# Two-layer hybrid decoder trunk: the second layer's mixer pacing, the order of its input blocks, S5's output products, and one modulation section

## The chip, the core and the metric

The kernel runs on one core of a Trainium2 chip as one launch. The metric is the device time of one execution in microseconds (us). TensorE (PE, with its weight loads shown apart as PEld), VectorE (DVE), ScalarE (ACT), GpSimd (POOL) and SyncE (SP) run their own instruction streams in order; the whole order is written out when the program is built.

## The reference, cut to what matters

```python
for l in range(2):
    sh1, sc1, gt1, sh2, sc2, gt2 = split(silu(c) @ ada_w[l] + ada_b[l], 6)   # "modulation"
    a = rms_norm(h, norm1_g[l]) * (1 + sc1) + sh1
    u_s5, r_q, r_k, r_v, r_g, w_q, w_k, w_v, m_cq, m_ckv, m_kr = split(a @ w_in[l])
    y = concat(s5(u_s5), retention(r_*), sliding_window(w_*), mla(m_*))      # 4 mixers, 512 wide each
    h = h + gt1 * (y @ w_out[l])
    a = rms_norm(h, norm2_g[l]) * (1 + sc2) + sh2
    h = h + gt2 * (square(relu(a @ mlp_w1[l])) @ mlp_w2[l])
out = rms_norm(h, final_norm_g)
# s5: u -> B u (complex, 16 tiles of 128 states) -> scan over 256 steps -> Re(C state) + d u -> gelu -> GLU
```

One sequence of 256 positions, width 2048, all float32. MLA is the latent attention (two low-rank projections, rotary, softmax), SWA the windowed attention with sinks, RET the retention mixer.

## The kernel before

**The data stream.** `make_plan` (L84) writes one list of items. A data item is a 128x1024 float32 slab of weights (128x640 for block K) that SP fetches from one packed stream, in list order. For an "in", "out", "w1" or "w2" item ScalarE rounds the slab to a high part `wH` and VectorE subtracts to get a low part `wL` (`prep`, L350); `NHL` = 3 such pairs exist, so both run up to three items ahead of TensorE, which then does three matmuls for each product (high by high, high by low, low by high). An "ad" item belongs to the modulation: VectorE multiplies the slab by silu(c) and sums it, TensorE does nothing. "aquad" entries make the normalised activations of 512 channels in stages: products with a diagonal matrix on TensorE, scale and shift on ScalarE, the low part on VectorE.

**The second layer's order.** Norm, then 56 "in" items, 8 for each of the blocks U (S5's input), C, K, Q, RQK, RV, RG; then 32 "out" items. Before, the items of U and C alternate by quarter of the contraction, and the aquads of quarters 1 to 3 are spread over these 16 items by `AQ` (L80). The sixteen "ad" items of the shift SH2 are merged into the 48 items from RV on.

**The mixers.** They are Python generators (`s5` L1423, `mla` L1021, `swa` L971, `ret` L1167) that issue a few instructions and yield. Each "in" or "out" item calls `step()` (L410) twice, once for each half of its matmuls; a call is named a slot here. A slot lets S5 go first, one turn, then the others one turn each, in rotation, until the `Meter` (L225) has counted more than the budget `BUD` (L252) in that slot: VectorE 3, ScalarE 3, TensorE 1.5 in the second layer. The meter counts 0.07 + 0.00104 n for a VectorE instruction on n elements per partition. Where a result is needed, `ysplit` (L799) calls `need` (L432), which calls `step()` until that mixer is done, with no data item in between: MLA is needed before the first output item, SWA before the third, S5 before the seventh, RET before the eleventh.

**S5.** For each of 8 pairs of state tiles: products with B (4 matmuls, `bu`), two turns that multiply by cosine and sine, a turn with half the scan and its carry, a turn with the other half, two turns that multiply back, and the output products of the pair (8 matmuls into the bank `yp`, L1514 to L1522), which are issued right after them. Every second pair then adds the skip term. Before the fifth pair seven turns make the tables' second half (`s5_steps`).

Of the kernel before, what the change touches and what calls it, by code (L numbers as in the profile page):

```python
# [13 lines left out]
ALU = mybir.AluOpType  # L14
# [33 lines left out]
def _merge(main, extra):  # L48
    out, e, n, m = [], 0, len(main), len(extra)
    for i, it in enumerate(main):  # L50
        out.append(it)
        want = (i + 1) * m // n
        out.extend(extra[e:want])
        e = want
    return out
# [9 lines left out]
def _ad_sec(l, s, n=16):  # L65
    return [("ad", l, s, j, hf) for j in range(n) for hf in range(2)] + [("modfin", l, s, n)]
# [10 lines left out]

AQ = sorted([(max(0, 2 * k - 1 + stage), k, stage) for k in range(6) for stage in range(3)], reverse=True)  # L80
AQ = [(at, 1 + k // 2, 2 * (k % 2), stage) for at, k, stage in AQ]


def make_plan():  # L84
    p = []
    for l in range(LAYERS):
# [26 lines left out]
        else:  # L113
            p += _gap(1, 1)
            rest = REST[1]
        if l == 1:
            pair = rest[:2]
            first = [("in", l, b, kq, hf) for kq in range(4) for b in pair for hf in range(2)]
            rest = first + [("in", l, b, kq, hf) for b in rest[2:] for kq in range(4) for hf in range(2)]
        else:  # L120
            rest = [("in", l, b, kq, hf) for b in rest for kq in range(4) for hf in range(2)]
        if l == 0:
            rest = _merge(rest, later[4:]) if rest else later[4:]
        QO = MIX[l]
        outs = [("out", l, q, nb, hf, q == QO[0] and hf == 0, q == QO[3] and hf == 1)
                for nbs in ((0, 1), (2,), (3,)) for q in QO for nb in nbs for hf in range(2)]
        if l == 1:
            for at, q, c, stage in AQ:
                rest.insert(at, ("aquad", l, 1, q, c, stage))
            at = rest.index(("in", l, "RV", 0, 0))  # L130
            ws = rest[at:] + outs
            ws = _merge(ws[:48], _ad_sec(1, SH2, 8)) + ws[48:]
            rest = rest[:at] + ws
            rest.insert(at - 4, ("csilu", l))
            rest.insert(at - 4, ("cload", l))
        else:
            rest += outs
            rest.insert(len(rest) - 4, ("csilu", l))
            rest.insert(len(rest) - 16, ("cload", l))
        at = rest.index(outs[0])  # L140
        rest[at:at] = [("hload", l), ("gput", l, GT1)]
        rest.insert(rest.index(outs[10]), ("gget", l, GT1))
# [8 lines left out]
        w += [("w1", l, nb, kq, hf) for nb in range(2, 16) for kq in range(4) for hf in range(2)]  # L151
        w += [("w2", l, kq, nb, hf) for kq in range(16) for nb in range(4) for hf in range(2)]
        if l == 0:
            ex = _ad_sec(0, GT2) + sum([_ad_sec(1, s, 8 if s == SH1 else 16) for s in (SC1, SH1, GT1, SC2)], [])
        else:
            ex = _ad_sec(1, GT2)
        ex.append(("cdone", l))
# [87 lines left out]
def trunk_kernel(ctx: ExitStack, tc: tile.TileContext, A, out):  # L245
# [3 lines left out]

    NHL, NS, LA = 3, 31, 4  # L250

    BUD = ((1, 1.5, 1), (3, 3, 1.5))  # L252
    cst = ctx.enter_context(tc.tile_pool(name="cst", bufs=1))
    hp = ctx.enter_context(tc.tile_pool(name="hp", bufs=1))
    whp = ctx.enter_context(tc.tile_pool(name="whp", bufs=NHL))
# [23 lines left out]
    def bank():  # L279
        assert banks, "no bank left"  # L280
        tag = banks.pop(0)
        uid[0] += 1
        t = ps.tile([128, 512], F32, tag=tag, name=f"p{uid[0]}")
        owner[id(t)] = (tag, t)
        return t
# [9 lines left out]
    def g_banks(n, reserve=2):  # L295
        while len(banks) < n + reserve:
            yield
# [97 lines left out]

    bud = [BUD[0]]

    def run_bg(name, gen):
        active.append((name, gen))

    rr, nslot, pace = [0], [0], [2]

    def step1(a):
        try:
# [5 lines left out]
    def step():  # L410

        v0, a0, p0 = V.t, ACT.t, PE.t
        lead = [a for a in active if a[0][0] in ("T", "S5")]
        rest = [a for a in active if a[0][0] not in ("T", "S5")]
        nslot[0] += 1
        if nslot[0] % pace[0]:
            return
        if rest:
            r = rr[0] % len(rest)
            rest = rest[r:] + rest[:r]  # L420
        for i, a in enumerate(lead + rest):
            if i >= len(lead):
                rr[0] += 1
            step1(a)
            if V.t - v0 > bud[0][0] or ACT.t - a0 > bud[0][1] or PE.t - p0 > bud[0][2]:
                break

    def g_wait(n):
        for _ in range(n):
# [993 lines left out]
    def s5(l):  # L1423
# [29 lines left out]
        yield from g_banks(2, 1)  # L1453
        nxt = bu(0)
        yield
        yp = None
        for p in range(8):
            pbs = nxt
            if p == 4:
# [19 lines left out]
            if p < 7:  # L1479
                yield from g_banks(2, 1)  # L1480
                nxt = bu(p + 1)
            mg = [mag[:, 2 * p + e:2 * p + e + 1].to_broadcast([128, 128]) for e in range(2)]
            for e in range(2):
                for r in range(2):
# [21 lines left out]
            for e in range(2):  # L1506
# [3 lines left out]
                V.tensor_tensor(P8[:, 0:4, :], w4, cosb, op=ALU.mult)  # L1510
                V.tensor_tensor(P8[:, 4:8, :], w4, sinb, op=ALU.mult)
                yield
            yield
            if p % 2 == 0:  # L1514
                yield from g_banks(1, 1)
                yp = bank()
            for n, (m, src) in enumerate(((0, 0), (0, 3), (1, 2), (1, 1))):
                for e in range(2):
                    i = 2 * p + e
                    p0, cs, o = 32 * (i % 4), slice(32 * i, 32 * i + 32), 256 * (n == 3)  # L1520
                    PE.matmul(yp[p0:p0 + 32, o:o + 256], lhsT=C[:, m, cs], rhs=W[2 + e][:, src, :],
                              start=n in (0, 3), stop=n in (2, 3), tile_position=(0, p0))  # L1522
            if p % 2 == 1:
                yield
                k = p // 2
                V.scalar_tensor_tensor(y[:, k, :], u[:, k, :], T["d"][:, 0, k:k + 1], yp[:, 0:256],
                                       op0=ALU.mult, op1=ALU.add)
                V.tensor_tensor(y[:, k, :], y[:, k, :], yp[:, 256:512], op=ALU.subtract)
                bfree(yp)
        free(C, bT, cos, sin, *W)  # L1530
        yield from g_slots(3)
        gw = [slot([128, 2, 512]) for _ in range(2)]
# [230 lines left out]
```

## Time and profile before

| | |
|---|---|
| median of 3 runs | 2331.61 us (2330.83 to 2331.77) |
| the profiled execution: time / span of its instructions | 2330.54 us / 2328.4 us |
| granted TensorE clock, mean | 0.991 |
| HBM traffic | 252 GB/s over the span |
| matmul records | 12150 |

The page of the profile gives the busy time of each engine. The granted clock is a share of full speed: 1.00 is the 2.4 GHz level and 0.50 the 1.2 GHz level, and a value between is a stretch that had both. An entry in brackets at the end of a timeline row is the engine's idle time just before that instruction and what released it. Two records stand for one float32 matmul (w by w), one for one matmul of the rounded parts.

### The profile page before, as it was taken

Reading aid. Unit: us, or ns where it says so; the run is one execution under the profiler, and the core shown is the slowest. Engines: PE = TensorE matmul, PEld = TensorE weight load, DVE = VectorE, ACT = ScalarE, POOL = GpSimd, SP = SyncE. Lnnn points to the kernel's source line nnn. Section 1 sums busy time; section 2 is a strip of 40 time slices with the busy share of each in tenths; the row PEclk is TensorE's granted clock in tenths of the full one; section 3 lists DMA queues with packets and bytes.
Section 4 is the critical chain, followed back from the end, with each engine's and each line's share of the span. In section 5 each row is a group of like instructions: output and inputs, shape, how many; then the busy total and the mean of one; then the engine's idle time right before and its main releaser. Section 6 shows DMA issues by size and latency. Waiting matters only on the chain.

```text
span 2328.4 us, 32118 instructions
## 1 busy us (share of the span) xinstructions
PE 2254.6 (97%) x12150; PEld 1809.9 (78%) x12150; DVE 1579.4 (68%) x2591; ACT 1016.7 (44%) x1378; POOL 40.9 (2%) x65
## 2 busy tenths in 40 slices
PE   6999999999999999999999889999999999999997
PEld 3775457889888888888878757778988888888885
DVE  5848764646878787889965987574576665545546
ACT  2352245544444444444444345544444444444443
POOL 0000000000000000000000000000000000000000
PEclk9999999999999999999999989999999999999999
DMA  9986677777888889998985314787667766667640
GB/s 380 408 329 244 253 290 269 273 272 260 281 280 286 271 307 334 339 335 296 342 315 196 97 57 154 262 320 277 215 223 236 233 214 202 216 215 221 219 146 36
DMA packets 162459, 588.23 MB, mean 253 GB/s; under 512 B 18448, under 2 KB 18672, under 8 KB 162304
## 3 DMA queue, kind: packets, MB, share of 16 engines
q1 hardware_dynamic: 156096, 563.79, 68.6%
q0 software_dynamic: 6208, 22.39, 2.9%
q8 instruction: 95, 1.56, 0.3%
q14 instruction: 60, 0.49, 0.1%
HBM read 581.88 MB, written 4.23 MB: 252 GB/s over the span
## 4 chain that ended last, share of the span: by engine, by line
PE 84%; DVE 7%; issue 4%; DMA 2%; ACT 2%; POOL 0%; POOLq 0%; ACTq 0%; SPq 0%; DVEq 0%
PE p L239 84%; DVE w L239 5%; DVE wL L239 2%; DMA w<-in_stream_dram 2%; ACT wH L239 1%; ACT w L239 1%; DVE s5i L239 0%; ACT a L239 0%; DVE a L239 0%; DMA gains<-in_gains_dram 0%; POOL nr L569 0%; ACT rjk L239 0%; DVE f L239 0%; POOL rss L1232 0%; POOL mss L1038 0%
## 5 line engine op out<-in xcount | busy, mean ns | idle before, releaser
L239 DVE TENSOR_TENSOR wL<-w,wH 128x1024 fp32r<-128x1024 f32 (+1 forms) x688 | 831.9, 1214 | 612.7 <-ACT wH L239 602.7
L239 ACT CAST wH<-w 128x1024 fp32r<-128x1024 f32 (+1 forms) x688 | 715.9, 1044 | 931.9 <-PE p L239 798.7
L239 PE MATMUL p<-wH,a 128*128 128x512 f32 (+1 forms) x3200 | 1008.5, 390 | 11.6 <-ACT wH L239 6.6
L239 PE MATMUL p<-a,wH 128*128 128x512 f32 (+1 forms) x2880 | 838.2, 357 | 3.9 <-DVE a L239 2.6
L239 PEld LDWEIGHTS p<-wH,a 128*128 128x128 f32 x3200 | 600.4, 188 | 163.3 <-issue 22.1
L239 PE MATMUL p<-a,wL 128*128 128x256 f32 x2336 | 657.9, 282 | 4.2 <-DVE wL L239 4.2
L239 PE MATMUL p<-wL,a 128*128 128x512 f32 (+1 forms) x1600 | 618.6, 387 | 4.0 <-DVE wL L239 4.0
L239 PEld LDWEIGHTS p<-a,wH 128*128 128x128 f32 x2880 | 506.5, 189 | 100.2 <-ACT wH L239 7.2
L239 PEld LDWEIGHTS p<-a,wL 128*128 128x128 f32 x2336 | 442.9, 190 | 4.8 <-DVE wL L239 4.8
L239 PEld LDWEIGHTS p<-wL,a 128*128 128x128 f32 x1600 | 301.7, 189 | 64.3 <-DVE wL L239 7.0
L239 PE MATMUL p<-w,w 128*32 128x512 f32 (+5 forms) x1464 | 244.6, 507 | 10.6 <-DVE w L239 8.5
L239 DVE CUSTOM_DVE_ANT_0 w<-w,w 128x1024 f32<-128x1024 f32 x192 | 233.8, 1218 | 0.0
L239 PEld LDWEIGHTS p<-w,w 128*32 128x32 f32 (+3 forms) x1464 | 97.5, 134 | 109.9 <-issue 58.5
L239 ACT COPY w<-p 128x256 f32<-128x256 f32 (+2 forms) x192 | 85.7, 461 | 122.1 <-PE p L239 121.5
L239 DVE TENSOR_TENSOR w<-p,w 128x256 f32<-128x256 f32 (+1 forms) x230 | 113.2, 533 | 12.7 <-PE p L239 12.6
L239 DVE TENSOR_TENSOR w<-w,w 128x512 f32<-128x512 f32 (+6 forms) x172 | 93.6, 564 | 7.6 <-ACT w L239 4.0
L239 DVE TENSOR_TENSOR a<-w,a 128x1024 fp32r<-128x1024 f32 (+2 forms) x78 | 71.4, 918 | 10.6 <-ACT a L239 10.3
L239 ACT ACTIVATE w<-w 128x512 f32<-128x512 f32 (+2 forms) x50 | 36.9, 742 | 64.5 <-DVE w L239 62.0
L239 ACT CAST a<-w 128x1024 fp32r<-128x1024 f32 (+1 forms) x58 | 53.1, 916 | 0.6
L239 ACT COPY apev<-p 128x512 f32<-128x512 f32 x24 | 14.0, 584 | 50.9 <-PE p L239 50.9
L239 DVE SCALAR_TENSOR_TENSOR w<-w 128x1024 f32<-128x1024 f32 x28 | 34.3, 1226 | 1.0
L239 PEld LDWEIGHTS p<-kc,apev 128*128 128x128 f32 x192 | 23.4, 191 | 13.4 <-issue 4.2
(163 smaller groups left out, 639.4 us busy)
## 6 DMA issues: line engine op xcount, KB each, us to landing
w<-in_stream_dram SPq DMA_DIRECT2D x1056, 512.0 KB, 4.9
w<-in_stream_dram SPq DMA_DIRECT2D x16, 320.0 KB, 9.8
w<-gd POOLq DMA_DIRECT2D x8, 512.0 KB, 5.4
w<-in_w_uq_dram POOLq DMA_DIRECT2D x6, 384.0 KB, 7.5
w<-in_xT_dram SPq DMA_DIRECT2D x4, 512.0 KB, 6.9
w<-in_glu_w_dram POOLq DMA_DIRECT2D x4, 512.0 KB, 6.4
w<-in_x_dram POOLq DMA_DIRECT2D x4, 512.0 KB, 7.5
w<-in_c_dram POOLq DMA_DIRECT2D x4, 512.0 KB, 7.2
```

Source lines behind the costliest of these rows:

```text
L239: return f(out, *a, **k)
```

## The change

Four edits, all of them about the second layer but the last, which moves work of the second layer into the first layer's MLP.

1. The second layer's budget is VectorE 1.2, with a debt: what a slot spent is carried, each slot takes 1.2 off, and while a debt is left the slot issues nothing.
2. U's eight items come first, then C's; the aquads go by `AQ1`, one stage for each item, so that they are through after the first items.
3. S5's output products of a pair are issued in the next pair, after that pair's B products; for each odd pair two yields stand between its products and the skip term.
4. SH2's sixteen "ad" items go into the list that is merged into the first layer's MLP. With them gone, "cload" and "csilu" (the silu(c) rows for "ad" items) stand 16 and 4 items before the end of the output items, as in the first layer.

```diff
-AQ = sorted([(max(0, 2 * k - 1 + stage), k, stage) for k in range(6) for stage in range(3)], reverse=True)
-AQ = [(at, 1 + k // 2, 2 * (k % 2), stage) for at, k, stage in AQ]
+def _aq(step):
+    p = sorted([(max(0, step * k - 1 + stage), k, stage) for k in range(6) for stage in range(3)], reverse=True)
+    return [(at, 1 + k // 2, 2 * (k % 2), stage) for at, k, stage in p]
+AQ1, AQ = _aq(1), _aq(2)
...
-        if l == 1:
-            pair = rest[:2]
-            first = [("in", l, b, kq, hf) for kq in range(4) for b in pair for hf in range(2)]
-            rest = first + [("in", l, b, kq, hf) for b in rest[2:] for kq in range(4) for hf in range(2)]
-        else:
-            rest = [("in", l, b, kq, hf) for b in rest for kq in range(4) for hf in range(2)]
+        rest = [("in", l, b, kq, hf) for b in rest for kq in range(4) for hf in range(2)]
...
-            for at, q, c, stage in AQ:
+            for at, q, c, stage in AQ1:
                 rest.insert(at, ("aquad", l, 1, q, c, stage))
-            at = rest.index(("in", l, "RV", 0, 0))
-            ws = rest[at:] + outs
-            ws = _merge(ws[:48], _ad_sec(1, SH2, 8)) + ws[48:]
-            rest = rest[:at] + ws
-            rest.insert(at - 4, ("csilu", l))
-            rest.insert(at - 4, ("cload", l))
-        else:
-            rest += outs
-            rest.insert(len(rest) - 4, ("csilu", l))
-            rest.insert(len(rest) - 16, ("cload", l))
+        rest += outs
+        rest.insert(len(rest) - 4, ("csilu", l))
+        rest.insert(len(rest) - 16, ("cload", l))
...
-            ex = _ad_sec(0, GT2) + sum([_ad_sec(1, s, 8 if s == SH1 else 16) for s in (SC1, SH1, GT1, SC2)], [])
+            ex = _ad_sec(0, GT2) + sum([_ad_sec(1, s, 8 if s in (SH1, SH2) else 16)
+                                       for s in (SC1, SH1, GT1, SC2, SH2)], [])
...
-    BUD = ((1, 1.5, 1), (3, 3, 1.5))
+    BUD = ((1, 1.5, 1, False), (1.2, 3, 1.5, True))
...
         if nslot[0] % pace[0]:
             return
+        debt[0] = max(0.0, debt[0] - bud[0][0]) if bud[0][3] else 0.0
+        if debt[0] > 0:
+            return
...
+        debt[0] = V.t - v0
...
+        def out_products(p):
+            if p % 2 == 0:
+                yield from g_banks(1, 1)
+                yp[0] = bank()
+            for n, (m, src) in enumerate(((0, 0), (0, 3), (1, 2), (1, 1))):
...
+            if p % 2 == 1:
+                yield
+                yield
...
+                bfree(yp[0])
...
             if p < 7:
                 yield from g_banks(2, 1)
                 nxt = bu(p + 1)
+            if p:
+                yield from out_products(p - 1)
             mg = [mag[:, 2 * p + e:2 * p + e + 1].to_broadcast([128, 128]) for e in range(2)]
...
-            yield
-            if p % 2 == 0:
-                yield from g_banks(1, 1)
-                yp = bank()
-            for n, (m, src) in enumerate(((0, 0), (0, 3), (1, 2), (1, 1))):
...
-            if p % 2 == 1:
-                yield
...
-                bfree(yp)
+        yield
+        yield from out_products(7)
```

## Rows read from the trace of the kernel before

**Rows 1.** the page: busy time of each engine, share of the span, instructions.

```profile
PE 2254.6 (97%) x12150; PEld 1809.9 (78%) x12150; DVE 1579.4 (68%) x2591; ACT 1016.7 (44%) x1378; POOL 40.9 (2%) x65
```

**Rows 2.** 10-us windows: start:end, length, busy (count) by engine, PEclk, DMA share.

```profile
1280.00:1290.00 10.00, 8.96 (x71) 6.99 (x70) 9.93 (x27) 1.51 (x3) 0.00 (x0) 1.00 0.32 104
1290.00:1300.00 10.00, 8.96 (x69) 6.56 (x67) 9.93 (x18) 2.78 (x3) 0.00 (x0) 1.00 0.32 107
1300.00:1310.00 10.00, 8.70 (x69) 7.37 (x69) 9.93 (x31) 3.74 (x11) 1.53 (x1) 1.00 0.16 53
...
1320.00:1330.00 10.00, 6.90 (x40) 4.32 (x39) 9.56 (x24) 1.04 (x1) 0.36 (x1) 0.83 0.32 105
...
1350.00:1360.00 10.00, 3.64 (x11) 2.30 (x10) 6.91 (x34) 4.42 (x19) 0.00 (x0) 0.72 0.07 12
1360.00:1370.00 10.00, 7.52 (x27) 3.90 (x27) 6.21 (x18) 7.49 (x13) 0.00 (x0) 0.60 0.29 107
```

**Rows 3.** chain of waits, 1200 to 1560 us: start, us, what.

```profile
1214.05 56.48 PE p L239 x376
...
1368.99 107.62 PE p L239 x506
```

**Rows 4.** timeline of VectorE, one pair of S5: start, us, instruction [idle before, releaser].

```profile
1282.46 1.28 DVE L239 TENSOR_TENSOR w<-p,w 128x512 f32<-128x512 f32 x2
...
1286.44 0.82 DVE L239 TENSOR_TENSOR wL<-w,wH 128x640 fp32r<-128x640 f32 x1
...
1291.71 2.49 DVE L239 TENSOR_TENSOR w<-w,w 128x512 f32<-128x512 f32 x4
```

**Rows 5.** timeline of PE: output products of S5's first and second pair.

```profile
1281.26 2.08 PE L239 MATMUL p<-w,w 128*32 128x256 f32 x14 [1.04 <-DVE w L239]
...
1293.65 2.08 PE L239 MATMUL p<-w,w 128*32 128x256 f32 x14 [0.58 <-DVE w L239]
```

**Rows 6.** timeline of PE: 512-column matmuls after a stall and later.

```profile
1357.11 0.80 PE L239 MATMUL p<-wH,a 128*128 128x512 f32 x1 [5.90 <-ACT wH L239]
...
1371.01 0.50 PE L239 MATMUL p<-wH,a 128*128 128x512 f32 x1
```

**Rows 7.** timeline of POOL: MLA's second weight load; the residual's reload.

```profile
1397.71 0.53 POOL L1093 DMA_DIRECT2D w<-in_w_ukv_dram  x1 [63.29 <-DVE wL L239]
...
1471.49 1.68 POOL L1619 DMA_DIRECT2D w<-hs  x3 [9.26 <-ACT w L239]
```

**Rows 8.** timeline of PE at the first output item.

```profile
1480.74 0.80 PE L239 MATMUL p<-wH,a 128*128 128x512 f32 x1 [2.66 <-ACT a L239]
```

**Rows 9.** timeline of ScalarE: MLA's softmaxes, exponentials and division.

```profile
1445.54 0.40 ACT L239 ACTIVATE w<-w,sxm 128x128 f32<-128x128 f32 x1 [1.04 <-DVE sxm L239]
...
1449.01 0.19 ACT L239 ACTIVATION_READ_ACCUMULATOR w<-w,sxm 128x1 f32 x1
...
1455.94 2.87 ACT L239 ACTIVATE w<-w,sxd 128x128 f32<-128x128 f32 x8
```

**Rows 10.** timeline of VectorE: the maxima of the same softmaxes, first and last.

```profile
1444.38 0.28 DVE L239 CUSTOM_DVE_ANT_0 w<-p,kc 128x128 f32<-128x128 f32 x1
...
1446.80 0.08 DVE L239 DVE_READ_ACCUMULATOR2_ANT sxm<- 128x1 f32 x1
```

**Rows 11.** timeline of ScalarE: a table load and what follows.

```profile
1477.24 1.28 ACT L239 ACT_TABLE_LOAD   x1
1478.53 1.09 ACT L239 ACTIVATE w<-p 128x512 f32<-128x512 f32 x2
```

**Rows 12.** timelines of POOL and VectorE: the end of RET's chain.

```profile
1513.88 2.50 POOL L1232 TENSOR_TENSOR rss<-rss,mexp 128x8 f32<-128x8 f32 x1 [33.35 <-DVE rss L239]
...
1516.41 2.19 DVE L239 SCALAR_TENSOR_TENSOR w<-w,rss,w 128x128 f32<-128x128 f32 x8 [0.42 <-POOL rss L1232]
```

**Rows 13.** a window of the first layer's MLP.

```profile
1000.00:1200.00 200.00, 199.08 (x875) 163.78 (x874) 174.71 (x293) 86.38 (x89) 2.13 (x4) 1.00 0.88 318
```

**Rows 14.** a 10-us window at the first layer's first output items.

```profile
370.00:380.00 10.00, 7.72 (x48) 6.40 (x47) 3.47 (x5) 4.16 (x8) 0.00 (x0) 1.00 1.03 415
```

More of the change, by code (lines that the diff above doesn't have):

```diff
@@ L399, in run_bg @@
         active.append((name, gen))
-    rr, nslot, pace = [0], [0], [2]
+    rr, nslot, pace, debt = [0], [0], [2], [0.0]
     def step1(a):
@@ L1455, in s5 @@
         yield
-        yp = None
+        yp = [None]
+        def out_products(p):
[3 more added lines that the diff above has]
+            for n, (m, src) in enumerate(((0, 0), (0, 3), (1, 2), (1, 1))):
+                for e in range(2):
+                    i = 2 * p + e
+                    p0, cs, o = 32 * (i % 4), slice(32 * i, 32 * i + 32), 256 * (n == 3)
+                    PE.matmul(yp[0][p0:p0 + 32, o:o + 256], lhsT=C[:, m, cs], rhs=W[2 + e][:, src, :],
+                              start=n in (0, 3), stop=n in (2, 3), tile_position=(0, p0))
+            if p % 2 == 1:
+                yield
+                yield
+                k = p // 2
+                V.scalar_tensor_tensor(y[:, k, :], u[:, k, :], T["d"][:, 0, k:k + 1], yp[0][:, 0:256],
+                                       op0=ALU.mult, op1=ALU.add)
+                V.tensor_tensor(y[:, k, :], y[:, k, :], yp[0][:, 256:512], op=ALU.subtract)
+                bfree(yp[0])
         for p in range(8):
@@ L1512, in s5 @@
                 yield
-            yield
-            if p % 2 == 0:
-                yield from g_banks(1, 1)
-                yp = bank()
-            for n, (m, src) in enumerate(((0, 0), (0, 3), (1, 2), (1, 1))):
[L1518 to L1522, printed above, removed]
-            if p % 2 == 1:
-                yield
[L1525 to L1528, printed above, removed]
-                bfree(yp)
+        yield
+        yield from out_products(7)
         free(C, bT, cos, sin, *W)
```

## The prediction

> **What bounds the kernel now.** I read the busy table first: TensorE is busy 97% of the span and VectorE 68% [rows 1], so the change can win back only stretches in which TensorE is kept waiting. Of the 10-us windows I then took those of the second layer, and there TensorE's gaps lie almost all in one place, the "in" items from K to RV [rows 2]. In the three windows from 1280 VectorE is busy 9.93 us of 10, while TensorE loses 1.04, 1.04 and 1.30 us; later it loses 3.10, 6.36 and 2.48 us, at a granted clock of 0.83, 0.72 and 0.60. The windows left out between them have no gap, so the idle time of 1280 to 1370 sums to 15.3 us. The chain of waits says the same: two long TensorE pieces, one that ends at 1270.5 and one that begins at 1369.0, and none of that length between [rows 3]. What fills VectorE there is S5: one pair takes from 1282.46 to 1294.20 with two weight subtractions of 0.8 us inside, so 10.2 us of its own [rows 4]. TensorE feels it twice: the output products wait for the last multiplication (1.04 and 0.58 us ahead of one pair's products each) [rows 5], and weight items wait for a rounded or subtracted slab that stands behind mixer work (5.90 us once), after which a 512-column matmul takes 0.80 us instead of 0.50, the 1.2 GHz level [rows 6].
>
> **What the stall is worth.** The granted clock gives the share at the lower level: 0.83 is 34% of the window, 0.72 is 56%, 0.60 is 80%. Half the busy time at that level is lost: 6.90 x 0.34 / 2 = 1.2, 3.64 x 0.56 / 2 = 1.0, 7.52 x 0.80 / 2 = 3.0, together 5.2 us [rows 2]. With the idle 15.3 us the stretch costs 20.5 us. That is all that edits 1 to 3 can take away there.
>
> **Edits 1 and 3, the in items.** In meter units a turn of S5 that multiplies costs 1.88, the first scan turn 1.38, the second 0.81, a turn that multiplies back 1.205. At 1.2 a slot the debt makes these 2, 2, 2, 1, 2 and 2 slots: 11 a pair. (1.205 misses one slot by 0.005.) From the third pair on each odd-numbered one (3, 5, 7) takes 13, since the late products yield twice. So S5 spends 8.3 units in 11 to 13 slots, about 0.7 a slot. Two slots are one item, so VectorE has 10.2 us of S5 and some 6 subtractions against 6 items of TensorE work; it falls behind no longer except in the K items, whose matmuls are shorter. The late output products find their operands ready, so their wait goes [rows 5]. I leave 4 us of stall (bounds 0 and 14, the second if VectorE still ends last through K): gain 16.5 us.
>
> **What is late next.** U complete after slot 16 lets S5 begin at 17. Pairs 1 to 4 take 46 slots, the tables' turns 12, pairs 5 and 6 take 24: slot 99; pair 7 takes 13. So when the 56 items, 112 slots, are used up, S5 stands at its seventh pair's end. The others are worse off. A slot in debt issues nothing at all, and a S5 turn over 1.2 closes its slot. Only the 0.81 turn, the turns without VectorE work and the four short table turns let others in: some 10 slots between K's end (slot 48) and 112, shared in rotation among MLA, SWA's two parts and RET. MLA alone needs 28 turns. Before, each slot had room for others, and MLA was so far that its second weight load went out at 1397.7, ahead of the residual's reload at 1471.5, which marks the first output item [rows 7]. After, nearly all of MLA, half of SWA, S5's eighth pair and its GLU are still to come when the first output item asks for MLA. I count about 50 calls of `step()` in that `need`, with no weight item between them. TensorE's work is the same, it only loses its cover. Three gaps follow.
> - S5's seventh pair still has 4 us on VectorE and the eighth 10.2 us [rows 4], 14.3 us together. TensorE has for them two sets of output products' worth of time (about 2.1 us each [rows 5]) and, by an estimate, 1 us of transposes for MLA and SWA: idle 9 us.
> - After that four chains interleave and TensorE is busy, until only the last softmaxes are left. MLA's two take 2.5 us of maxima [rows 10], 3.7 us of exponentials and 2.9 us of division [rows 9], and the scores and transposes of one run beside the softmax of the other; with SWA's last block I estimate 8 us of idle, near the 9.1 that the three make in series.
> - MLA's result is rounded (1.0 us) and subtracted (1.2 us) with nothing else to run: 2 us. Before, the same place shows 2.66 us [rows 8].
>
> That is 19 us of idle time. Each of four gaps is followed by matmuls at the lower level; at the first output item before, 3.4 us ran so, as its first matmul of 0.80 us shows [rows 8], costing 1.6 us: 6 us for four. From 25 us the 2.7 + 1.6 that before already pays there go off: cost 20.7 us. Bounds: 6, if the interleaving covers all but the last hop; 38, if MLA's turns run one after the other.
>
> The table loads in it: a load takes 1.28 us and the next instruction begins 0.01 us later, the one before it ended 0.02 us earlier [rows 11], so gelu, sigmoid and exponentials cost about 3.8 us of ScalarE, partly inside the idle time above. The Trainium skill (ScalarE: Activation LUTs, What ACT_TABLE_LOAD costs) adds about 1.38 us of drain to each switch, 2.66 us in all; by that three switches on the path would add some 4 us, and the forecast would be 2345. The row shows no such drain, so I take the load alone.
>
> **RET.** It begins when MLA is done or ten slots of memory are free, so a few turns later than before, and the eleventh output item asks for it. Its end is a chain: ScalarE's squares, 2.50 us on POOL, 2.19 us on VectorE [rows 12], then transposes. Before, items lay beside it; after, I count three forced calls: 5 us (bounds 0 and 9).
>
> **Edit 2.** With an aquad stage for each item, the low parts of a half quarter are issued one item ahead of their use instead of two. That item's matmuls hide them; if they don't, TensorE waits at each of six halves for less than one VectorE instruction of 128x512 (half of the 1.28 us that two take [rows 4]): 0, at most 4 us.
>
> **Edit 4.** Sixteen multiplications of 1.2 us leave the items from RV on. There TensorE has little to gain: under 2 us of gaps after 1490, so -1 (0 to -2). In the first layer's MLP they join a VectorE that is busy 174.7 of 200 us, while TensorE idles 0.9 [rows 13]: 3% more load, +1 (0 to 4). "csilu" now puts a table load and two 1 us silus ahead of the last weight casts: +1 (0 to 3).
>
> **The sum.** -16.5 + 20.7 + 5 - 1 + 1 + 1 = +10.2 us. The profiled execution took 2330.5 us (span 2328.4 and 2.1 around it), which gives 2340.7; the median of the runs lies 1.1 us above it, so 2341.8: **2341 us**, 0.4% slower.
>
> **The rivals.**
> - *The rush at the output items is covered* (not slower). Mechanism: in the forced calls S5, MLA, SWA and RET take turns, each fills the others' waits, and TensorE runs through. It decides from where the rush costs less than 10.5 us. For it: in the first layer, where S5 also goes first and shuts others out, TensorE loses only 2.3 us in the window of the first output items [rows 14]. Against it: there the budget carries no debt and modulation items lie between. With 6 us of rush, 2 of RET and the rest as above: -16.5 + 6 + 2 + 1 = -7.5, at best -14: 2317 to 2325, say **2322 us**.
> - *The ration does not free VectorE.* The debt counts in meter units, 8.3 for a pair that takes 10.2 us, and in the K items VectorE still ends last. For it: 9.93 of 10 us there [rows 2]. Against it: S5's turns come half as often. The gain falls to 6 us, the rush stays: +20, **2352 us**.
> - *The rush has no cover.* MLA's 26 turns in series, at the lower clock: +38 in place of 20.7, **2358 us** and above. For it: one softmax with nothing beside it cost 5.90 us [rows 6]. Against it: SWA and GLU's 6 us.
>
> **How the numbers follow.** Forecast 0.44, covered rush 0.36, ration without effect 0.10, no cover 0.10. A change under 0.2% (4.7 us, 2327 to 2336) is about what these runs cannot tell from none. The forecast's own range is 2331 to 2351: 0.65 slower, 0.33 same, 0.02 faster. The covered rush: 0.85 faster, 0.15 same. The last two: 0.95 slower. Together faster 0.32, same 0.21, slower 0.47. The range 2316 to 2358 leaves out one in ten on each side. The forecast is the likeliest case, not the middle.
>
> **What would show it.** Right: no wait of output products for VectorE's multiplications; VectorE well under 9.9 of 10 us from 1280 on; the residual's reload some 65 us earlier than 1471, then about 75 us almost without weight matmuls and with gaps of 3 to 6 us, MLA's second weight load inside them; the first output matmul near 1484. Wrong: weight matmuls spread evenly up to the output items, MLA's second weight load well ahead of the reload, or a rush without gaps. The first layer's MLP should end within 4 us of before; if not, edit 4 was mis-sized.

## The result and the profile after

The changed kernel takes **2361.61 us** (median of 4 runs, 2350.12 to 2363.21) against 2331.69 for the kernel before beside it: ratio 1.0119, 95% interval [1.0103, 1.0135], 30 us or 1.2% slower. The forecast was 2341, the range 2316 to 2358. The direction was right, the size was not: the result lies above the range.

TensorE's row, which answers to [rows 1], is 20 us busier with the same 12150 matmuls. They ran slower; no work was added.

```profile
PE 2274.6 (96%) x12150; PEld 1826.9 (77%) x12150; DVE 1579.2 (67%) x2591; ACT 1020.1 (43%) x1379; POOL 44.3 (2%) x65
```

Where in the program it goes is read from one instruction that occurs once a norm: POOL's small power "nr". Timeline of POOL, kernel before (start, us, instruction, idle before it and its releaser):

```profile
480.03 1.62 POOL L569 TENSOR_TENSOR nr<-nr,mexp 128x2 f32<-128x2 f32 x1 [69.34 <-DVE nr L239]
1212.11 1.56 POOL L569 TENSOR_TENSOR nr<-nr,mexp 128x2 f32<-128x2 f32 x1 [4.59 <-DVE nr L239]
1587.79 0.71 POOL L569 TENSOR_TENSOR nr<-nr,mexp 128x2 f32<-128x2 f32 x1 [70.34 <-DVE nr L239]
2319.25 0.71 POOL L569 TENSOR_TENSOR nr<-nr,mexp 128x2 f32<-128x2 f32 x1 [112.67 <-DVE nr L239]
```

The same four in the changed kernel:

```profile
497.74 1.63 POOL L567 TENSOR_TENSOR nr<-nr,mexp 128x2 f32<-128x2 f32 x1 [79.40 <-DVE nr L232]
1232.19 1.56 POOL L567 TENSOR_TENSOR nr<-nr,mexp 128x2 f32<-128x2 f32 x1 [4.59 <-DVE nr L232]
1621.39 1.56 POOL L567 TENSOR_TENSOR nr<-nr,mexp 128x2 f32<-128x2 f32 x1 [69.57 <-DVE nr L232]
2351.61 0.71 POOL L567 TENSOR_TENSOR nr<-nr,mexp 128x2 f32<-128x2 f32 x1 [112.67 <-DVE nr L232]
```

The differences of neighbouring marks give four stages: the first layer's mixers 480.0 to 497.7 (+17.7), its MLP 732.1 to 734.5 (+2.4), the second layer's mixers 375.7 to 389.2 (+13.5), its MLP 731.5 to 730.2 (-1.2). Sum +32.4 for these two profiled executions. More than half is lost in the first layer's mixers, for which the prediction has no term.

**The second layer.** The 10-us windows of the changed kernel that answer to [rows 2] (columns as there); the stage begins 20 us later than before:

```profile
1300.00:1310.00 10.00, 10.00 (x88) 9.32 (x88) 9.93 (x20) 3.97 (x5) 0.00 (x0) 1.00 0.46 139
1310.00:1320.00 10.00, 10.00 (x88) 9.19 (x85) 9.97 (x25) 3.90 (x5) 0.00 (x0) 1.00 0.26 79
1320.00:1330.00 10.00, 10.00 (x85) 9.39 (x85) 9.60 (x15) 3.14 (x3) 0.00 (x0) 1.00 0.45 152
...
1350.00:1360.00 10.00, 7.76 (x27) 5.78 (x27) 7.08 (x30) 4.68 (x12) 0.00 (x0) 0.83 0.19 66
1360.00:1370.00 10.00, 8.85 (x40) 6.96 (x39) 9.86 (x16) 3.22 (x4) 0.00 (x0) 1.00 0.26 88
...
1420.00:1430.00 10.00, 7.09 (x34) 5.51 (x32) 7.64 (x23) 6.35 (x11) 2.21 (x5) 1.00 0.32 105
1430.00:1440.00 10.00, 5.18 (x26) 2.42 (x26) 9.93 (x29) 2.44 (x9) 0.47 (x1) 0.83 0.30 107
1440.00:1450.00 10.00, 8.43 (x36) 4.43 (x36) 4.12 (x10) 3.38 (x4) 1.08 (x2) 0.83 0.19 53
...
1470.00:1480.00 10.00, 7.92 (x26) 5.04 (x26) 1.76 (x12) 6.68 (x19) 0.53 (x1) 0.79 0.08 23
1480.00:1490.00 10.00, 10.00 (x21) 5.20 (x22) 1.84 (x13) 0.00 (x0) 0.00 (x0) 0.50 0.08 32
1490.00:1500.00 10.00, 5.53 (x8) 1.30 (x7) 1.32 (x8) 4.42 (x19) 0.00 (x0) 0.50 0.16 52
1500.00:1510.00 10.00, 8.13 (x37) 6.71 (x38) 2.25 (x4) 6.85 (x15) 0.00 (x0) 0.67 0.54 189
...
1540.00:1550.00 10.00, 5.95 (x35) 4.88 (x33) 1.73 (x5) 5.33 (x19) 1.97 (x2) 1.00 0.31 94
```

The in items lose 2.24 and 1.15 us of idle time in the two windows from 1350, and 1.04 after 1400, where before they lost 15.3: most of the stall is gone. VectorE is as full as before in the first three windows shown (9.93, 9.97 and 9.60 us of 10), but TensorE no longer waits there. In the stall's place stands the rush: the mixers' turns that are forced at the first output item with no weight item between them. POOL's timeline, which answers to [rows 7, 12]: the residual's reload begins at 1420.86, and MLA's second weight load comes 41 us after it, where it had been 74 us ahead of it.

```profile
1420.86 0.59 POOL L1624 DMA_DIRECT2D w<-hs  x1 [78.22 <-DVE sxd L232]
...
1462.06 0.53 POOL L1091 DMA_DIRECT2D w<-in_w_ukv_dram  x1 [14.14 <-PE p L232]
...
1548.03 1.66 POOL L1230 TENSOR_TENSOR rss<-rss,mexp 128x8 f32<-128x8 f32 x1 [69.71 <-DVE rss L232]
```

The large gaps of TensorE in it, to be set beside [rows 5, 8]; the row of 1509.67 is the first output item, 29 us later than before, 20 of them from the later start:

```profile
1430.79 0.62 PE L232 MATMUL p<-w,w 128*32 128x256 f32 x2 [3.70 <-DVE w L232]
...
1440.98 0.62 PE L232 MATMUL p<-w,w 128*32 128x256 f32 x2 [4.42 <-DVE w L232]
...
1474.72 2.52 PE L232 MATMUL p<-kc,w 128*128 128x128 f32 x8 [1.87 <-ACT w L232]
...
1500.12 3.81 PE L232 MATMUL p<-kc,w 128*128 128x128 f32 x12 [4.58 <-ACT w L232]
...
1509.67 0.50 PE L232 MATMUL p<-wH,a 128*128 128x512 f32 x1 [1.75 <-ACT a L232]
...
1550.22 2.22 PE L232 MATMUL p<-kc,w 128*128 128x128 f32 x8 [4.28 <-DVE w L232]
```

**The first layer** shows a rush as well. Windows of the changed kernel around its first output items, to be set beside [rows 14]; the kernel before has a granted clock of 1.00 from 340 to 420:

```profile
350.00:360.00 10.00, 10.00 (x47) 5.77 (x45) 6.49 (x18) 3.36 (x9) 0.00 (x0) 0.81 0.27 105
360.00:370.00 10.00, 10.00 (x37) 5.63 (x36) 3.43 (x5) 5.19 (x14) 0.53 (x1) 0.85 0.61 209
370.00:380.00 10.00, 8.49 (x52) 4.99 (x53) 3.78 (x14) 7.56 (x20) 2.10 (x4) 1.00 0.91 322
380.00:390.00 10.00, 9.75 (x37) 8.08 (x36) 1.25 (x4) 2.75 (x6) 0.00 (x0) 0.51 0.42 154
390.00:400.00 10.00, 7.97 (x21) 5.69 (x22) 2.33 (x4) 2.98 (x4) 0.00 (x0) 0.67 0.70 264
```

By the working of the prediction (half the busy time at the lower level) these five windows lose 10.8 us to the clock and 3.8 to idling; before, 350 to 400 lost 3.0 us, all idle. About 2 of the 17.7 are not the change's: the first load of MLA's weights, ahead of which nothing was changed, begins at 137.60 before and at 139.95 here, and in all kernels below between 137.6 and 142.6.

### The profile page after: what moved, and what is told of

Read it like the earlier page. It is cut to its first block, busy times and chain, and to the rows that moved or that the text cites. A ratio compares the mean times of both kernels' runs of the same rounds, so it can differ in the third digit from the quotient of the medians.

```text
span 2361.1 us, 32118 instructions
## 1 busy us (share of the span) xinstructions
PE 2274.6 (96%) x12150; PEld 1826.9 (77%) x12150; DVE 1579.2 (67%) x2591; ACT 1020.1 (43%) x1379; POOL 44.3 (2%) x65
## 5 line engine op out<-in xcount | busy, mean ns | idle before, releaser
L232 PE MATMUL p<-wH,a 128*128 128x512 f32 (+1 forms) x3200 | 998.5, 389 | 8.2 <-ACT wH L232 3.6
L232 PEld LDWEIGHTS p<-wL,a 128*128 128x128 f32 x1600 | 302.6, 189 | 72.6 <-DVE wL L232 14.5
L232 PE MATMUL p<-w,w 128*32 128x512 f32 (+5 forms) x1464 | 251.4, 522 | 10.6 <-DVE w L232 9.3
L232 PEld LDWEIGHTS p<-w,w 128*32 128x32 f32 (+3 forms) x1464 | 104.6, 141 | 111.5 <-issue 65.1
L232 DVE TENSOR_TENSOR w<-w,w 128x512 f32<-128x512 f32 (+6 forms) x172 | 94.0, 565 | 11.8 <-ACT w L232 8.2
L232 DVE TENSOR_TENSOR a<-w,a 128x1024 fp32r<-128x1024 f32 (+2 forms) x78 | 71.4, 918 | 18.6 <-ACT a L232 18.3
L232 DVE TENSOR_TENSOR mod<-p,modb 128x2 f32<-128x2 f32 (+1 forms) x32 | 5.1, 158 | 50.1 <-PE p L232 50.1
L232 PE MATMUL p<-kc,w 128*128 128x128 f32 x140 | 25.6, 310 | 12.6 <-ACT w L232 6.5
```

Of the source, the lines that this page charges most:

```text
L232: return f(out, *a, **k)
```

## The experiments

Stage lengths are from the profiled execution of each kernel, totals are medians of the timed runs with their ratio to the kernel before beside them. Edits are numbered as in the change: 1 the ration, 2 U first, 3 the late output products, 4 the shift products and csilu out of the second layer's mixers. Each stage length is that of one execution. Where the first layer is as before, its mixers take 480.0 to 485.1 us, and what the second mixers and the total differ by from the kernel before agrees within 3 us, so 3 us or less between two stage lengths can be noise. The profiled execution of f is its fastest, 6 us below its median (2335.2 against 2341.5), and its stage lengths gain from that.

| kernel | first mixers | second mixers | total us | ratio, 95% |
|---|---|---|---|---|
| before | 480.0 | 375.7 | 2331.7 | |
| changed: 1, 2, 3, 4 | 497.7 | 389.2 | 2361.6 | 1.0119 [1.0103, 1.0135] |
| a_l0_early: 1, 2, 3 in layer two only, 4 | 482.7 | 387.2 | 2342.9 | 1.0051 [1.0036, 1.0066] |
| b_late_only: 3 | 498.2 | 389.3 | 2363.4 | 1.0139 [1.0122, 1.0156] |
| f_late_blank: b and one empty turn a pair | 482.9 | 379.1 | 2341.5 | 1.0051 [1.0033, 1.0069] |
| d_no_ration: a without 1 | 480.5 | 369.8 | 2324.6 | 0.9972 [0.9962, 0.9981] |
| e_debt_s5_only: a, debt holds S5 alone | 481.4 | 369.5 | 2328.3 | 0.9990 [0.9981, 1.0000] |
| i_ration125: a, ration 1.25 | 480.5 | 375.1 | 2330.8 | 0.9996 [0.9986, 1.0005] |
| v_debt15: a, ration 1.5 | 480.7 | 374.1 | 2328.6 | 0.9990 [0.9981, 0.9999] |
| t_budget15: d, budget 1.5, no debt | 482.4 | 381.9 | 2339.4 | 1.0034 [1.0022, 1.0046] |
| o_budget2: d, budget 2, no debt | 481.1 | 366.2 | 2321.7 | 0.9958 [0.9942, 0.9975] |
| k_uc_mixed: d without 2 | 485.1 | 387.4 | 2342.1 | 1.0049 [1.0033, 1.0065] |
| m_u_first: d without 3 | 483.1 | 373.4 | 2328.2 | 0.9989 [0.9979, 0.9998] |
| n_sh2_back: d without 4 | 481.1 | 379.0 | 2334.3 | 1.0009 [1.0000, 1.0018] |
| q_u_first_only: 2 | 481.2 | 381.8 | 2336.3 | 1.0024 [1.0015, 1.0033] |
| s_sh2_only: 4 | 481.7 | 376.3 | 2332.6 | 1.0008 [0.9999, 1.0018] |
| h_nr_blank: d and one empty turn a pair | 480.2 | 388.5 | 2344.1 | 1.0054 [1.0038, 1.0070] |
| u_csilu_early: d, csilu back ahead of RV | 480.2 | 375.7 | 2331.4 | 1.0001 [0.9991, 1.0010] |

**Where the late products cost.** The generator of S5 is shared, so edit 3 acts in both layers. a_l0_early gives the first one its old order back:

```diff
+        late = l == 1
...
-            if p:
+            if p and late:
                 yield from out_products(p - 1)
...
+            if not late:
+                yield
+                yield from out_products(p)
```

> The changed kernel with one thing taken back: in the first layer S5's output products stand in their own pair again, as before; the second layer keeps all of the change. Theory 1 (the late output products also act in the first layer, which the prediction overlooked, and cost some 17 us there): the second norm of the first layer comes back from 497.7 to 480 +- 3 us, the total falls by 15 to 18 us to 2343 to 2348 us. Theory 2 (the first layer's 17.7 us are a clock state of that execution and no edit's doing): the total stays at 2350 to 2363 us.

The first mixers fall from 497.7 to 482.7, their MLP to 732.3, and the total to 2342.9: theory 1, at the low edge of its band. So 19 of the 30 us are the first layer's share of edit 3, and what is left is the forecast's 2341 within 2 us.

b_late_only does the reverse, the kernel before with edit 3 and nothing else:

```diff
+            if p:
+                yield from out_products(p - 1)
...
-            yield
-            if p % 2 == 0:
...
+        yield
+        yield from out_products(7)
```

> The kernel before with only the late output products, in both layers. Theory 1: the first layer's second norm moves from 480 to 495 +- 5 us; in the second layer the waits of output products go and 0 to 8 us are won; total 2338 to 2349 us. Theory 2: the first layer stays at 480 +- 3 us and the total is 2323 to 2333 us.

It costs 18 us in the first layer and 14 in the second: as slow as the whole change, without ration. For the first layer that is theory 1; in the second, where theory 1 had 0 to 8 us won, and in the total it missed.

The reason, in the first layer, lies in the turns. In its old place the block has an empty turn ahead of it in every pair (the list of S5's turns above leaves it out): S5 issues nothing and its slot is free for MLA, SWA and RET. In the late order this turn is gone, and of the two yields of an odd pair only one makes an empty turn, since the products fill the other. Two pairs have one empty turn instead of two; with the turn of 0.81 units, which stays under the first layer's budget of 1, that is 3 open turns instead of 4. f_late_blank puts one empty turn a pair back into b:

```diff
                 V.tensor_tensor(P8[:, 4:8, :], w4, sinb, op=ALU.mult)
                 yield
+            yield
```

> The kernel before with the late output products in both layers and one empty turn at the end of each of S5's pairs. Theory T (the late products cost time by taking empty turns from S5's pair, so that the other mixers get fewer turns and more of them is left for the output items): both layers recover, first layer's second norm 480 to 486 (498.2 without the empty turn), second layer's stretch 372 to 380 (389.3 without), total 2328 to 2342 us. Rival D (the late products themselves, by the order on VectorE or the banks that they hold): first layer stays at 494 or more, total 2355 us or more.

The first mixers are back at 482.9, the second at 379.1, as theory T has it. In the first layer MLA shows it. Its second weight load in the timelines of POOL, kernel before, changed kernel, and f (both layers):

```profile
198.41 0.60 POOL L1093 DMA_DIRECT2D w<-in_w_ukv_dram  x1 [39.07 <-PE p L239]
```

```profile
213.16 0.59 POOL L1091 DMA_DIRECT2D w<-in_w_ukv_dram  x1 [51.47 <-PE p L232]
```

```profile
199.37 0.60 POOL L1093 DMA_DIRECT2D w<-in_w_ukv_dram  x1 [39.07 <-PE p L239]
...
1310.78 0.60 POOL L1093 DMA_DIRECT2D w<-in_w_ukv_dram  x1
```

For the second layer this account is not shown. In b MLA is not late there; its second weight load goes out at

```profile
1385.01 0.53 POOL L1093 DMA_DIRECT2D w<-in_w_ukv_dram  x1 [18.54 <-DVE wL L239]
```

which is 153 us after the stage began (1231.55), against 186 us in the kernel before, and yet the stage is 13.6 us longer. That f's empty turn gives 10 of them back is measured; by which way it does is open.

**What the ration costs.** d_no_ration takes edit 1 out of a; e_debt_s5_only keeps the debt, but a slot in debt holds back S5 alone; i_ration125 and v_debt15 change the ration only.

```diff
 # d_no_ration
-    BUD = ((1, 1.5, 1, False), (1.2, 3, 1.5, True))
+    BUD = ((1, 1.5, 1, False), (3, 3, 1.5, False))
 # e_debt_s5_only
         if debt[0] > 0:
-            return
+            lead = []
...
-        debt[0] = V.t - v0
+        debt[0] += V.t - v0
 # i_ration125, v_debt15
-    BUD = ((1, 1.5, 1, False), (1.2, 3, 1.5, True))
+    BUD = ((1, 1.5, 1, False), (1.25, 3, 1.5, True))
...
+    BUD = ((1, 1.5, 1, False), (1.5, 3, 1.5, True))
```

> The first kernel of this call (first layer as before) without the ration: second layer's budget 3, 3, 1.5 and no debt; U first, late output products and SH2's items in the MLP stay. Theory A (the ration makes the rush at the first output item, which costs the second layer its 13.5 us): MLA's second weight load is again ahead of the residual's reload, the stretch from norm to norm of the second layer is 365 to 376 us (before 375.7, changed 389.2), total 2318 to 2332 us. Theory B (U first and the late products cost it, whatever the pace): the stretch stays over 383 us, total 2340 us or more.

> The first kernel of this call with one edit of the ration: a slot in debt holds back S5 alone, the other mixers still get their turn. Theory A (what hurts is that MLA and SWA get no turn, not that VectorE is thinned): MLA's second weight load goes out before the residual's reload, the rush shrinks, the second layer's stretch is 360 to 375 us, total 2316 to 2331 us. Rival (S5's own lateness sets the rush, since S5 gets no faster): the stretch stays at 383 to 390 us, total 2340 to 2348 us.

> The changed kernel with the first layer as before (2342.9 us), ration 1.25 in place of 1.2. Theory S (the slots' arithmetic: at 1.2 a turn of 1.205 takes two slots, at 1.25 one, so a pair takes 9 or 11 slots in place of 11 or 13 and S5 is through some 16 slots earlier): fewer calls are forced at the first output item, the second layer's stretch falls from 387 to 376 to 382, total 2331 to 2338 us. Rival (the ration's size matters little, skipped slots as such do the harm): stretch 385 to 389, total 2340 to 2345 us.

> The changed kernel with the old products' place in the first layer, and the ration 1.5 with its debt in place of 1.2 (1.2 gave 387.2 us of mixer stage, 1.25 gave 375.1, no ration 369.8). Theory 1 (slots in debt are what costs; at 1.5 only the two multiplying turns skip a slot, so a pair takes 8 slots, after 11 and 9): stage 369 to 374, total 2324 to 2330. Rival (any debt shuts out MLA long enough for the rush): 375 or more, total 2330 or more.

Without the ration the second mixers take 369.8 us, 17.4 less than in a, and the kernel is 7 us faster than before: theory A, with MLA's second weight load (1340.41) again ahead of the reload (1482.89). The 10-us windows say what the ration trades, idle time and clock by the prediction's working. From 1230 to 1400 a loses 6.9 us and d 18.7, nearly the 20.5 of the kernel before; from 1400 to the end of the stage a loses 32.6 and d 3.9. So the ration takes 11.8 us out of the stall and adds 28.7 behind it; the difference of 16.9 agrees with the 17.4 of the stages. Two windows of d, one in what is left of its stall, one at its first output item:

```profile
1320.00:1330.00 10.00, 5.53 (x44) 4.96 (x41) 9.79 (x22) 4.38 (x7) 0.00 (x0) 1.00 0.17 53
...
1480.00:1490.00 10.00, 6.85 (x30) 5.05 (x29) 5.86 (x12) 6.95 (x13) 4.27 (x6) 1.00 0.82 322
```

At 1.25 the turns of 1.205 take one slot and no longer two, a pair takes 9 slots instead of 11 by the meter's arithmetic, and 12 of the 17.4 us come back, a microsecond more than theory S had; at 1.5 it is 8 slots and 374.1 us, at the edge of what was expected. e's stage is as short as d's, as theory A has it (its total is 3.7 us longer), although its weight load still follows the reload, which theory A had not:

```profile
1423.27 0.60 POOL L1630 DMA_DIRECT2D w<-hs  x1 [120.66 <-PE p L232]
...
1437.99 0.55 POOL L1091 DMA_DIRECT2D w<-in_w_ukv_dram  x1
```

So the order of these two does not set the price: e has it the wrong way round and is fast, and h below has the load 154 us ahead and is slow. e differs from a in that a slot in debt lets the others have their turns, and in that its debt adds up. The price is paid where the slots in debt issue nothing for anyone.

t_budget15 and o_budget2 make the budget smaller without debt:

```diff
-    BUD = ((1, 1.5, 1, False), (3, 3, 1.5, False))
+    BUD = ((1, 1.5, 1, False), (1.5, 3, 1.5, False))
...
+    BUD = ((1, 1.5, 1, False), (2, 3, 1.5, False))
```

> As the kernel without ration, the second layer's VectorE budget of a slot 1.5 units, no debt (2 units gave 366.2 us of mixer stage, 3 units 369.8). Theory 1 (without debt a smaller budget only closes a slot after a big turn, it skips none: it goes on gaining or stays): 363 to 368, total 2318 to 2324. Rival (the budget itself takes turns from MLA and SWA and makes the rush): 371 or more, total 2326 or more.

> As the kernel without ration, the second layer's VectorE budget of a slot 2 units in place of 3, no debt. Theory 1 (a smaller budget that forgets its overdraft closes a slot after one big turn, which spreads S5 a little and leaves others their turns): stage 364 to 370, total 2319 to 2325. Rival (any smaller ration takes turns from MLA and makes a rush): 374 or more, total 2329 or more.

At 2 the stage is 366.2 us, the best of all, as theory 1 has it, and at 1.5 it is 381.9, the rival's. Between the two lies S5's multiplying turn, 1.88 units: at 1.5 it closes its slot and nobody else is called, at 2 the slot stays open for one more. That this is the whole cause is argued. That the debt makes 1.5 better (374.1) than 1.5 without it was not expected, and its cause is open.

**The edits one by one.** For edits 2, 3 and 4 the second mixers were measured in all eight combinations, without ration: none 375.7; 2 alone 381.8; 3 alone 389.3; 4 alone 376.3; 2 and 3 379.0; 2 and 4 373.4; 3 and 4 387.4; all three 369.8 (3 alone is b, with edit 3 in both layers). Four runs of it:

```diff
 # k_uc_mixed: U and C by turns and AQ as before, else d
+            pair = rest[:2]
+            first = [("in", l, b, kq, hf) for kq in range(4) for b in pair for hf in range(2)]
...
 # m_u_first: output products early in both layers, else d
-        late = l == 1
+        late = False
 # n_sh2_back: SH2, csilu and cload back in the second layer's items, else d
+            ws = _merge(ws[:48], _ad_sec(1, SH2, 8)) + ws[48:]
...
 # q_u_first_only: the kernel before with U first and AQ1
-            for at, q, c, stage in AQ:
+            for at, q, c, stage in AQ1:
...
```

> The kernel without ration (2324.6 us) with the items of U and C alternating again as before, so S5 begins some 12 slots later. Theory U (U first is what lets S5 go late without a rush): second layer's stretch from 369.8 to 378 to 390, total 2332 to 2345 us, with more forced calls at the output items. Rival (U first does nothing, the gain is edit 4's or the late products'): stretch 366 to 373, total 2321 to 2328 us.

> No ration, output products in their old place in both layers, U first, shift products in the first layer's MLP. Theory 1 (late products take turns from MLA and SWA in the second layer too, so taking them back helps): second layer's mixer stage 360 to 368 us (369.8 with late products), total 2315 to 2323. Rival (in the second layer the late products take away the waits behind VectorE and that pays for the turns): 374 to 382, total 2328 to 2337.

> As the kernel without ration (late products in the second layer alone, U first), with the shift products and csilu put back among the second layer's items. Theory 1 (edit 4 is worth no more than 2 us either way, as the prediction has it): second layer's mixer stage 368 to 373, first MLP 732.0 to 732.3, total 2323 to 2328. Rival (the products held VectorE while the output items wait): stage 376 or more, total 2331 or more.

> The kernel before with edit 2 alone: U as the first block, with a part of the modulation quads at each item. Theory 1 (an earlier S5 is the one part of the change that gains, about 6 to 18 us): stage 358 to 370, total 2314 to 2326. Rival (it gains only with the late products or with the shift products gone): 374 to 380, total 2330 to 2336.

U first costs 6 us alone and gains 17.6 beside edits 3 and 4. The late products cost 13.6 alone and gain 3.6 once U is first and edit 4 is in (373.4 to 369.8). So k is theory U's, q came out beyond its rival's band and m at the edge of its rival's. Edit 4 gains 9.2 there (n), not 2: the rival again. The medians of the totals say the same: 4.6 for U first alone, -17.5 beside 3 and 4, -3.6 for the late products and -9.7 for edit 4 in the company named. Why the edits need each other is not shown: in q S5's first output products come 15 us sooner in their stage than before, and q is slower.

s_sh2_only and u_csilu_early ask what edit 4 is:

```diff
 # s_sh2_only: the kernel before with
+            ex = _ad_sec(0, GT2) + sum([_ad_sec(1, s, 8 if s in (SH1, SH2) else 16)
+                                       for s in (SC1, SH1, GT1, SC2, SH2)], [])
... (and without the SH2, csilu and cload lines of the second layer, as in the change)
 # u_csilu_early: d with
-        rest.insert(len(rest) - 4, ("csilu", l))
+        rest.insert(at - 4 if l == 1 else len(rest) - 4, ("csilu", l))
... (cload likewise; at is the place of RV's first item)
```

> The kernel before with edit 4 alone (shift products into the first layer's MLP, csilu and its load at the end). Theory 1 (the shift products and the early csilu each cost the mixers something, whatever the order of the blocks): second layer's mixer stage 366 to 371 us (375.7 before), total 2321 to 2327. Rival (edit 4 pays only once U goes first, since before that the stalls lie elsewhere; the prediction had -1): 373 to 376, total 2328 to 2332.

> As the kernel without ration (369.8 us mixer stage, 2324.6), with csilu and its load alone put back ahead of the RV items; the shift products stay in the first layer's MLP. Theory 1 (csilu's two table changes in the middle of the mixers hold up ScalarE's exponentials and casts, and this is most of edit 4's 9 us): stage 375 to 379, total 2330 to 2335. Rival (it is the sixteen products on VectorE): 369 to 372, total 2323 to 2327.

Alone edit 4 does nothing (+0.6, a quarter of a microsecond above the rival's band). Of its 9.2 us beside 2 and 3, csilu's place makes 5.9 (the low end of theory 1), the products about 3 (by the medians 6.9 and 2.8). But most of the cost isn't at csilu (its table load is at 1383.07). It shows some 100 us later, at the first output item: the timelines of TensorE and ScalarE in u

```profile
1489.22 0.79 PE L233 MATMUL p<-wH,a 128*128 128x512 f32 x1 [5.75 <-ACT a L233]
```

```profile
1485.71 1.28 ACT L233 ACT_TABLE_LOAD   x1
1487.01 1.09 ACT L233 ACTIVATE w<-p 128x512 f32<-128x512 f32 x2
```

show ScalarE with a table load and two evictions ahead of MLA's rounding, and TensorE waiting 5.75 us. (The Trainium skill, ScalarE: Activation LUTs, What ACT_TABLE_LOAD costs, adds a drain of about 1.38 us to such a load; the next instruction begins 0.02 us after it here, 0.01 in [rows 11].) In d the same load and evictions stand ahead of the rounding, so they alone are not the difference, and the wait is 2.63 (timelines of ScalarE and TensorE):

```profile
1481.87 1.28 ACT L232 ACT_TABLE_LOAD   x1
```

```profile
1485.37 0.50 PE L232 MATMUL p<-wH,a 128*128 128x512 f32 x1 [2.63 <-ACT a L232]
```

In d two weight casts stand between RET's squares ahead of that load, in u none does. 3.1 of the 5.9 us are this wait; behind it u has a granted clock of 0.77 and 0.89 in the windows from 1482 and 1492, where d has 1.00, which is some 2 us more. That what was moved early changed only which turns fell together at the end is argued.

h_nr_blank adds the empty turn of f to d:

```diff
+            yield
             if not late:
-                yield
                 yield from out_products(p)
```

> The kernel without ration (2324.6 us; first layer as before, second layer U first, late products, SH2's items in the MLP) with one empty turn at the end of each pair in the second layer. Theory T: more turns for MLA, SWA and RET and a thinner VectorE, so the second layer's stretch falls from 369.8 to 360 to 367, total 2314 to 2322 us. Rival: S5 gets later by 8 turns and its tail meets the output items, stretch 370 to 378, total 2325 to 2333 us.

Both expectations missed: 388.5 us. Free turns are no good in themselves. The added ones bring MLA forward (second weight load at 1319.65, in d at 1340.41) and delay S5, as the rival says. S5's last output products in the timelines of TensorE, d and h:

```profile
1404.74 1.92 PE L232 MATMUL p<-w,w 128*32 128x256 f32 x16
```

```profile
1436.38 1.92 PE L232 MATMUL p<-w,w 128*32 128x256 f32 x16
```

From 1220 to 1420 h loses 33.2 us of idle time and clock, d 18.7; from 1420 to the end of the stage 10.9 and 3.9. That S5's delay is what costs them is argued.

## Why the prediction was wrong

**The step that failed** is the one that took edits 1 and 3 as edits to the in items of the second layer. For edit 1 that holds: the first layer's budget is unchanged and has no debt. For edit 3 it does not: the change to `s5(l)` has no condition on the layer. The prediction cites the first layer's mixers as evidence for the covered rush [rows 14], "in the first layer, where S5 also goes first and shuts others out, TensorE loses only 2.3 us", and gives them no term. They cost 17.7 us in the profiled execution, 15 by a (497.7 against 482.7), and 19 of the median total (2361.6 against 2342.9). Without this the forecast was 2 us off (2342.9; its own sum is 2341.8). That it came so near is in part luck: the terms below come to 6 us more than the stage, and what makes up for them is not known.

Within the second layer the steps stand so:

- *The stall goes, gain 16.5, 4 left.* Right, and a sign of it was not: the windows from 1350 to 1370 keep 3.4 us of idle time and 1.3 of clock, with 1.0 after 1400 5.7 in all, and no output product waits there. But VectorE is not well under 9.9 us of 10 in the K items.
- *Rush, idle 19 us in three gaps.* Right: 18.3 us from 1420 to 1511 (2.9 + 4.8 + 1.6 + 2.1 + 4.5 + 1.9, and 0.5 after 1510), with gaps of 3.7, 4.4 and 4.6 us, for S5's last pairs and for MLA's softmax. From the reload to the first output item it lasts 89 us, not 75.
- *6 us for the clock.* Mis-sized: by the same working the windows from 1430 to 1510 lose 14.5 us (0.9 + 1.4 + 1.7 + 5.0 + 2.8 + 2.7). The four windows from 1470 to 1510 make 12 of it. The prediction let each gap be followed by a few slow matmuls; after the one of 1.87 us some 20 us of them followed.
- *RET +5.* Right in the changed kernel: 4.05 us of idle time from 1540, and 1.7 for the clock behind it. In a, with the same second layer, the wait is 1.57 and the clock stays up, so the size is not steady.
- *Edit 3, the wait of the output products goes.* No such wait is left in the changed kernel's in items. But the edit's price is not this wait: in the second layer it cost 13.6 us alone (b) and gained 3.6 beside 2 and 4.
- *Edit 2: 0.* Wrong: +6 alone, -17.6 beside edits 3 and 4. The prediction priced its instructions; that its worth lies in when S5 begins is argued.
- *Edit 4: -1 and +1.* Its MLP term was right, 732.1 to 732.3 in a and 734.5 in the changed kernel, inside its bounds. The mixers' term was mis-sized in d: -9.2. In the changed kernel itself it was not measured.

These terms make more than the stage: 14.8 less in the in items, 28.5 more in the rush than the 4.3 that before pays there, 5.9 for RET, together +19.6 against +13.5. The windows are cut at 10 us and the ends of matmuls are modelled; some 6 us stay unassigned.

Of the rivals, "the ration does not free VectorE" is out by its price, since the stall went, though VectorE is as full as before through K. "Covered rush" is out in both layers. The rush's 28.5 us lie between the forecast's 20.7 and the 38 of "no cover". That the ration trades the stall for a rush was foreseen, and a against d bears it out; the trade costs 17.4 us, and without the ration most of the stall stays (18.7 us) and the kernel is faster all the same.

## What to carry to other kernels

When a shared generator is edited, list every place that runs it before pricing any. In a scheduler that lets several streams take turns, count turns, not only instructions: a place that issues nothing is where the others run, and more of them can cost as well as gain (f, h). An edit that moves a stream's start can be worth +6 or -18 us by what stands beside it, so measure edits in pairs; here U first with late products in the second layer only, edit 4 and a budget of 2 gives 2321.7 us, faster than both kernels (0.9958 [0.9942, 0.9975]).

## What the runs showed of the hardware

The clock fell with no gap ahead of it. In the first layer of the changed kernel TensorE's last wait before 354 is at 317.70, and yet MLA's scores (timeline of TensorE) change level in mid-row:

```profile
354.50 0.48 PE L232 MATMUL p<-krT,w 64*128 64x128 f32 x2
355.33 0.49 PE L232 MATMUL p<-krT,w 64*128 64x128 f32 x2
356.17 0.72 PE L232 MATMUL p<-krT,w 64*128 64x128 f32 x2
357.54 0.79 PE L232 MATMUL p<-krT,w 64*128 64x128 f32 x2
```

0.79 us a pair of records is the 1.2 GHz level, 0.48 the 2.4. Ahead of these rows TensorE ran, from 350.38, 16 records of 128x256 and 8 of one column, without a weight item. In the second layer, after the gap of 1.87 us ahead of 1474.72, it stayed at the lower one (0.50) from 1480 to 1490 in a window where TensorE is busy 10.00 of 10 us. In the kernel before, where weight items stand just ahead of the first layer's scores and behind them, the same pairs take

```profile
335.35 0.48 PE L239 MATMUL p<-krT,w 64*128 64x128 f32 x2
```

So next to weight items these scores ran at full clock, and without them some ran at half. To be without weight items is not enough for it: from 1450 to 1470 the changed kernel ran mixer matmuls alone, most of them in

```profile
1450.27 13.65 PE L232 MATMUL p<-w,w 128*128 128x256 f32 x62
```

at a granted clock of 1.00. What lets the clock fall in the scores was not tried.
